# A larger share of gathered rows beside the kept blocks, and the gate's preparation spread over fifty blocks with gathers beside it

## The chip, the cores and the metric

The kernel runs on one core of one Trainium2 chip. The metric is the device time of one launch in microseconds (us); lower is better. A core has TensorE (PE in the rows), VectorE (DVE), ScalarE (ACT), GpSimd (POOL) and SyncE (SP). Each takes its own instructions strictly in order, and they meet through semaphores. Transfers issued by SP go through one queue, those issued by POOL through another, and both are served by the same 16 DMA engines.

## What is computed

One layer of an encoder for 512 tokens of width 1024, all in float32. The reference, cut to what matters here:

```python
h = h + mixed @ w_out                       # attention and recurrence, first part of the kernel
xn2 = rms_norm(h, norm_ffn_g)
# PEER: 8 heads pick 16 of 128 x 128 experts each, so 128 experts for a token
def block(args):
    xb, ib, gb = args
    ue = exp_u[ib]
    logits = jnp.einsum('td,tkd->tk', xb, ue)
    act = jax.nn.gelu(logits) * gb
    ve = exp_v[ib]
    return jnp.einsum('tk,tkd->td', act, ve)
h = h + peer(xn2)
xn3 = rms_norm(h, norm_ple_g)
gate = jax.nn.sigmoid(xn3 @ ple_w_gate)
h = h + gate * (p @ ple_w_proj)
out = rms_norm(h, final_norm_g)
```

## The kernel before

The tokens are four tiles of 128. The experts of the first three tiles are worked out densely: a loop over 128 blocks of 128 experts makes all logits (the U loop, line 1017), and a second loop over the 128 blocks adds up the values (the **V loop**, line 1174). The fourth tile is done by **rows**: for each of its tokens' 128 choices, POOL gathers one row of `exp_u` or `exp_v` for each of the 128 tokens (`gather`, line 893, an indirect transfer of 512 KB into a tile named `rr` or `xn`), and DVE either multiplies it with the tile's activations (a u row, line 926) or adds it to `h` (a v row, line 933). There are 128 u rows and 128 v rows, handed out by the generator `rows` in units of cost 1.15.

The work beside the loops is paced by objects of the class `Background`: `run(share)` adds the share to a debt and draws steps from a generator until the debt is used up. In the V loop `bg` is what is left of the rows, and `prep` is `prepare()`, which loads the gate's weights. One V block consists of:

- `v_prep` (line 1047), one block ahead: the block's weights are multiplied out (`am`, line 1057) and split into a high and a low part (`ah` on ACT, `al` on DVE, lines 89 and 91).
- the rows of `exp_v` for the block are loaded by SP (`r`), and split likewise into `rh` on ACT and `rl` on DVE.
- `v_mm`: 18 matmuls into the accumulators `acc`, three for each pair of parts (lines 96 to 98).
- a share of the background: 1.2 (`BG_V`), for the rows, or from block 60 (`PREP`) until it is done for `prep`, in place of the rows.

The pools give `rh`, `rl`, `ah` and `al` three buffers each, so DVE can be at most two blocks ahead of PE.

For 26 of the blocks (`KEEP`; in the V loop's order those at 6 to 31) the logits stay on chip. For the others `lg` is read back, 192 KB a block.

`prepare()` costs 19.9 units in all: 0.6, then the loads and splits of `pT` and `w_proj` (four tiles), eight small products `psp` of six matmuls each, and eight loads and splits of `w_gate`. Each load goes by POOL's queue into a tile `w` that takes one of the four `rr` buffers, the same that gathers use, and is split by ACT and then DVE into `wg` (line 91 again, called W below).

After the V loop each of the four tiles is finished by `finish` (line 1129): norm, transposes (`turn`), 48 gate matmuls of 512 columns or their equal, sigmoid, product, final norm, store. The fourth tile can start there only when its last row is added. `bg.run(1e9)` at line 1229 draws all rows that are left.

A scheduler sets the order of instructions on each engine when the kernel is built, and the chip follows that order.

Of the kernel before, what the change touches and what calls it, by code (L numbers as in the profile page):

```python
# [39 lines left out]
KEEP = 26  # L40
G_SCALE = 2.0 ** 14
RO_AT = [2, 1, 1, 1, 1, 1, 1, 0, 0, 1, 0, 0, 1, 0, 0, 1, 0, 0, 1, 1, 9]
TOP_FIRST, TOP_THEN, MAKE, SIDE_1, SIDE, BG_V, HOT_DVE, PREP, SIDE_2 = 2.2, 1.0, 0.5, 0.6, 1.2, 1.2, 4, 60, 2.1
LAST = 3
N_HOT = 13
N_AT = 15, 17, 17
# [13 lines left out]
def trunk(ctx, tc, x, xT, pT, pos, w_lru, w_qkv, w_out, w_q, keys, wab, w_gate, w_proj,  # L60
# [85 lines left out]
    with ExitStack() as st:  # L146
# [129 lines left out]
        for ct in range(8):  # L276
# [12 lines left out]
            if ct < 4:  # L289
# [16 lines left out]
                for da in range(4):  # L306
                    i = da * 4 + ct
# [677 lines left out]
    order = [(J0 + i) % P for i in range(P)]  # L985
    feed = [ut[j].rearrange("p k e -> p (k e)") for j in range(P)] + [v[j * P:(j + 1) * P, :] for j in order]
    ahead = []
    kept = {}

    def advance():  # L990
        while feed and len(ahead) < 3:
            ahead.append(row_load(feed.pop(0)))
# [24 lines left out]
    for j in range(P):  # L1017
# [3 lines left out]
        else:  # L1021
            if j == P - KEEP:
                top.run(1e9)
            i = j - (P - KEEP)
# [22 lines left out]
    def v_prep(i):  # L1047
        j = order[i]
        gj = gcs[i // JC][:, :, i % JC, :]
        lg = kept.get(j)  # L1050
        if lg is None:
            lg = up.tile([P, NU], F32, tag="lg", name="lg")
            nc.sync.dma_start(lg, ld[j])
        if i + JC < P:
            weights(i // JC + 1, i % JC, vp)
        am = vp.tile([P, NTB, TB], F32, tag="am", name="am", bufs=1)
        nc.vector.tensor_mul(am, lg.rearrange("p (b t) -> p b t", t=TB), gj)  # L1057
        am = am.rearrange("p b t -> p (b t)")
        ah = vp.tile([P, NV], R, tag="ah", name="ah", bufs=LAST)
        al = vp.tile([P, NV], R, tag="al", name="al", bufs=LAST)  # L1060
        split(am, ah, al)
        return ah, al

    def v_mm(i, t, vh, vl, ah, al):
        tt = slice(t * P, (t + 1) * P)
        for n in range(2):
            ns = slice(n * T, (n + 1) * T)
            mm3(acc[t][n], ah[:, tt], al[:, tt], vh[:, ns], vl[:, ns], i == 0, i == P - 1)
# [13 lines left out]
    def load_gains():  # L1082

        both = vp.tile([P, 2, D], F32, tag="gc", name="gains")
        gains.extend([both[:, 0, :], both[:, 1, :]])
        for i in range(2):
            nc.sync.dma_start(gains[i], row[:, 256 + (i + 1) * D:256 + (i + 2) * D].to_broadcast([P, D]))

    def prepare():
        late_room()  # L1090
        yield 0.6
        for t in range(NT):
            for n in range(2):
                ns = slice(n * T, (n + 1) * T)
                psp = psu.tile([P, T], F32, tag="psl", name="psp")

                ph, pl = wg4[0][:, 0:2, 0:T], wg4[2][:, 0:2, 0:T]
                wph, wpl = wg4[0][:, 2:4, :], wg4[2][:, 2:4, :]
                if t == 0 and n == 0:
                    got = []  # L1100
                    for k in range(2):
                        w = gp.tile([P, D], F32, tag="rr", name="w")
                        nc.gpsimd.dma_start(w[:, 0:T], pT[k * P:(k + 1) * P, :])
                        got.append((w[:, 0:T], ph[:, k, :], pl[:, k, :]))
                        w = gp.tile([P, D], F32, tag="rr", name="w")
                        nc.gpsimd.dma_start(w, w_proj[k * P:(k + 1) * P, :])
                        got.append((w, wph[:, k, :], wpl[:, k, :]))
                        yield 0.3
                    yield 1.2
                    for g_ in got:  # L1110
                        split(*g_)
                        yield 0.6
                    yield 0.6
                tt = slice(t * P, (t + 1) * P)
                for k in range(2):
                    mm3(psp, ph[:, k, tt], pl[:, k, tt], wph[:, k, ns], wpl[:, k, ns], k == 0, k == 1)
                nc.scalar.copy(pp[0][:, t, ns], psp)
                yield 0.5

        got = []  # L1120
        for k in range(DK + 3):
            if k < DK:
                got.append(gp.tile([P, D], F32, tag="rr", name="w"))
                nc.gpsimd.dma_start(got[k], w_gate[k * P:(k + 1) * P, :])
            if k >= 3:
                split(got[k - 3], wg(k - 3, 0), wg(k - 3, 1))
            yield 1.2 if k >= 3 else 0.3
# [41 lines left out]
    bg = Background(side.gen)  # L1169
    prep = Background(prepare())  # L1170
# [3 lines left out]
    for i in range(P - LAST + 1):  # L1174
        advance()
        if i + 1 < P:
            vn.append(v_prep(i + 1))
        if i == P - JC:
            load_gains()
        if i == P - LAST:  # L1180
            break
        rhl, ahl = ahead.pop(0), vn.pop(0)
        for t in range(ND_V):
            v_mm(i, t, *rhl, *ahl)
        if i >= PREP and not prep.done:
            prep.run(BG_V)
        else:
            bg.run(BG_V)
    for i in range(P - LAST + 2, P):
        vn.append(v_prep(i))  # L1190
    prep.run(1e9)
# [111 lines left out]
```

## Time and profile before

| | us |
|---|---|
| median of 3 runs (1502.62 to 1505.04) | 1504.44 |
| the profiled execution's own time | 1502.74 |
| its span, first to last instruction | 1501.0 |
| V loop on PE, first to last accumulating matmul | 898.47 to 1437.35 |
| after it, to the end of the span | 63.65 |

The profile is of one execution. Times in rows are counted from the start of the span; the share of busy time is an average over stages that differ. A timeline row gives the start, the duration, the engine, the line, what is written from what, and in brackets how long the engine was idle just before and what ended that.

### The profile page before, as it was taken

What the parts mean: (1) busy time and instruction counts of PE and PEld (TensorE: products, weight loads), DVE (VectorE), ACT (ScalarE), POOL (GpSimd) and SP (SyncE); (2) the same over time, 40 slices, a digit from 0 to 9 for tenths busy, and PEclk for the clock granted to TensorE, in tenths of its full rate; (3) what the DMA queues carried; (4) which work ended last, traced back from release to release, by engine and by line L of the source; (5) the groups of instructions that cost most, each with busy time, mean ns of one, the idle gap of its engine ahead of it and who ended that gap; (6) DMA issues with size and microseconds to landing.
All of it is one profiled execution on the core that took longest, in us unless ns stands there. A gap on an engine that the chain in (4) does not pass through costs nothing.

```text
span 1501.0 us, 22206 instructions
## 1 busy us (share of the span) xinstructions
PE 1464.1 (98%) x7907; PEld 1294.7 (86%) x7907; DVE 1257.0 (84%) x2481; ACT 741.1 (49%) x1059; POOL 428.6 (29%) x320
## 2 busy tenths in 40 slices
PE   8999999999899999999999989999999999999996
PEld 6887678899899999999999987888888888888875
DVE  7686987789999999999878757788887588878895
ACT  7974754354555654565455533333333453333345
POOL 0000000010223374235333344344443014344450
PEclk9999999999999999999999999999999999999998
DMA  7223022156789898889998799989999789999971
GB/s 257 61 94 127 15 86 88 43 195 229 239 294 335 285 347 327 305 296 345 370 330 300 266 321 340 321 300 328 360 373 359 248 280 351 366 353 357 322 227 64
DMA packets 169199, 394.21 MB, mean 263 GB/s; under 512 B 15360, under 2 KB 90880, under 8 KB 166016
## 3 DMA queue, kind: packets, MB, share of 16 engines
q1 hardware_dynamic: 112336, 207.52, 41.1%
q0 software_dynamic: 38464, 140.00, 26.4%
q10 hardware_dynamic: 18288, 45.27, 7.8%
q8 instruction: 62, 1.02, 0.3%
q14 instruction: 49, 0.40, 0.1%
HBM read 345.41 MB, written 47.32 MB: 262 GB/s over the span
## 4 chain that ended last, share of the span: by engine, by line
PE 66%; DVE 21%; ACT 4%; issue 4%; DMA 3%; SPq 1%; DVEq 0%; ACTq 0%
PE acc L98 11%; PE acc L97 11%; PE acc L96 11%; PE psl L96 6%; PE psl L97 6%; PE psl L98 6%; DVE rl L91 4%; PE pg L855 2%; DVE rr L926 2%; PE ps L96 2%; PE ps L98 2%; PE ps L97 2%; DVE h L933 1%; DMA r<-in_v_dram 1%; SPq L1000 1%
## 5 line engine op out<-in xcount | busy, mean ns | idle before, releaser
L89 ACT ACTIVATE rh<-r 128x1024 fp32r<-128x1024 f32 x256 | 270.8, 1059 | 423.1 <-PE psl L97 188.1
L91 DVE TENSOR_TENSOR rl<-r,rh 128x1024 fp32r<-128x1024 f32 x256 | 312.2, 1220 | 95.5 <-ACT rh L89 93.4
L96 PE MATMUL psl<-x2h,rh 128*128 128x384 f32 x1024 | 348.2, 340 | 7.4 <-ACT keep L660 5.0
L98 PE MATMUL psl<-x2h,rl 128*128 128x384 f32 x1024 | 344.3, 336 | 3.6 <-DVE rl L91 3.6
L97 PE MATMUL psl<-x2l,rh 128*128 128x384 f32 x1024 | 343.9, 336 | 0.0
L98 PE MATMUL acc<-rh,al 128*128 128x512 f32 x768 | 299.8, 390 | 1.1 <-DVE al L91 1.1
L96 PE MATMUL acc<-rh,ah 128*128 128x512 f32 x768 | 299.4, 390 | 0.7 <-ACT ah L89 0.7
L97 PE MATMUL acc<-rl,ah 128*128 128x512 f32 x768 | 299.4, 390 | 0.3 <-DVE rl L91 0.3
L894 POOL DMA_INDIRECT rr<-in_u_dram,qidx x84 | 123.0, 1465 | 382.0 <-DVE rl L91 180.7
L894 POOL DMA_INDIRECT rr<-in_v_dram,qidxv x82 | 150.8, 1839 | 187.7 <-DVE rl L91 163.9
L96 PEld LDWEIGHTS psl<-x2h,rh 128*128 128x128 f32 x1024 | 193.0, 189 | 8.9 <-ACT keep L660 5.3
L98 PEld LDWEIGHTS psl<-x2h,rl 128*128 128x128 f32 x1024 | 193.2, 189 | 4.6 <-DVE rl L91 4.5
L97 PEld LDWEIGHTS psl<-x2l,rh 128*128 128x128 f32 x1024 | 193.3, 189 | 0.0
L98 PEld LDWEIGHTS acc<-rh,al 128*128 128x128 f32 x768 | 144.5, 188 | 31.8 <-DVE al L91 1.9
L96 PEld LDWEIGHTS acc<-rh,ah 128*128 128x128 f32 x768 | 144.6, 188 | 31.2 <-ACT ah L89 1.1
L97 PEld LDWEIGHTS acc<-rl,ah 128*128 128x128 f32 x768 | 144.4, 188 | 30.6 <-DVE rl L91 0.7
L89 ACT ACTIVATE ah<-am 128x384 fp32r<-128x384 f32 x128 | 66.3, 518 | 94.9 <-DVE am L1057 61.5
L933 DVE SCALAR_TENSOR_TENSOR h<-rr,qg,h 128x1024 f32<-128x1024 f32 x82 | 104.9, 1279 | 3.7 <-DMA rr<-in_v_dram,qidxv 3.7
L926 DVE CUSTOM_DVE_ANT_0 rr<-rr,xn 128x1024 f32<-128x1024 f32 x84 | 102.1, 1217 | 6.0 <-DMA rr<-in_u_dram,qidx 6.0
L894 POOL DMA_INDIRECT xn<-in_u_dram,qidx x44 | 68.6, 1559 | 110.7 <-DVE rl L91 92.7
L894 POOL DMA_INDIRECT xn<-in_v_dram,qidxv x46 | 74.8, 1627 | 88.8 <-DVE rl L91 81.4
L858 ACT COPY sg<-pg 128x512 f32<-128x512 f32 x96 | 95.8, 1107 | 1.0 <-ACT sc L695 0.4
(342 smaller groups left out, 2275.5 us busy)
## 6 DMA issues: line engine op xcount, KB each, us to landing
r<-in_ut_dram SPq DMA_DIRECT2D x128, 512.0 KB, 4.8
r<-in_v_dram SPq DMA_DIRECT2D x128, 512.0 KB, 6.8
gd<-sg ACTq DMA_DIRECT2D x24, 1024.0 KB, 7.5
gc<-gd SPq DMA_DIRECT2D x128, 192.0 KB, 7.7
ld<-lg ACTq DMA_DIRECT2D x102, 192.0 KB, 5.0
lg<-ld SPq DMA_DIRECT2D x102, 192.0 KB, 6.3
w<-in_w_qkv_dram SPq DMA_DIRECT2D x12, 512.0 KB, 3.6
w<-in_w_out_dram SPq DMA_DIRECT2D x8, 512.0 KB, 3.8
```

The costliest lines, as they stand in the source:

```text
L89: nc.scalar.activation(hi, src, AF.Copy, scale=1.0 if scale is None else scale)
L91: return nc.vector.tensor_sub(lo, src, hi.bitcast(F32))
L96: nc.tensor.matmul(ps, lhsT=lh, rhs=rh, start=first, stop=False)
L97: nc.tensor.matmul(ps, lhsT=lh, rhs=rl, start=False, stop=False)
L98: nc.tensor.matmul(ps, lhsT=ll, rhs=rh, start=False, stop=last)
L855: nc.tensor.matmul(pg[:, i - q, :], lhsT=o1[:, i // 2, :, i % 2], rhs=o2[part][:, i // 2, :, i % 2], start=part == 0, stop=part == 1)
L858: nc.scalar.copy(sg[:, :, s0:s0 + 4].rearrange("p j t -> p t j"), pg)
L894: g = nc.gpsimd.indirect_dma_start(out=dst, out_offset=None, in_=table, in_offset=bass.IndirectOffsetOnAxis(ap=idx, axis=0))
L926: behind(nc.vector.tensor_tensor_reduce(rr, rr, xn[:, t, :], 1.0, 0.0, ALU.mult, ALU.add, act[:, k % 16:k % 16 + 1]))
L933: behind(nc.vector.scalar_tensor_tensor(h[:, t, :], rr, qg[:, t, k:k + 1], h[:, t, :], op0=ALU.mult, op1=ALU.add))
L1000: nc.sync.dma_start(gcs[-1][:, b0:b1], gd[b0:b1, :, j * TB:(j + JC) * TB].rearrange("b p (j t) -> p b j t", t=TB))
```

## The change

Three numbers and two calls change. The preparation begins at block 40 in place of 60, at a share of 0.4 a block in place of 1.2, and rows go on beside it at 1.0 a block. Beside blocks that are kept on chip the rows' share is 1.4 in place of 1.2.

```diff
-TOP_FIRST, TOP_THEN, MAKE, SIDE_1, SIDE, BG_V, HOT_DVE, PREP, SIDE_2 = 2.2, 1.0, 0.5, 0.6, 1.2, 1.2, 4, 60, 2.1
+TOP_FIRST, TOP_THEN, MAKE, SIDE_1, SIDE, BG_V, HOT_DVE, PREP, SIDE_2 = 2.2, 1.0, 0.5, 0.6, 1.2, 1.2, 4, 40, 2.1
+
+BG_K, BG_P, PREP_V = 1.4, 1.0, 0.4
...
         if i >= PREP and not prep.done:
-            prep.run(BG_V)
+            prep.run(PREP_V)
+            bg.run(BG_P)
         else:
-            bg.run(BG_V)
+
+            bg.run(BG_K if order[i] in kept else BG_V)
```

What this does to the order shows on POOL and DVE. Line numbers of the changed kernel are two higher than before.

POOL, from where the gate's weights are loaded, before (`w` are these loads, `rr` and `xn` gathered rows):

```order
L1103 DMA w<-in_pT_dram 128x512
L894 DMA xn<-in_u_dram,qidx 128x1024
L1106 DMA w<-in_w_proj_dram 128x1024
L1103 DMA w<-in_pT_dram 128x512
L1106 DMA w<-in_w_proj_dram 128x1024
L1124 DMA w<-in_w_gate_dram 128x1024 x8
L894 DMA rr<-in_u_dram,qidx 128x1024 x2
```

and after, the loads of `w_gate`:

```order
L1126 DMA w<-in_w_gate_dram 128x1024 x2
L896 DMA xn<-in_v_dram,qidxv 128x1024
L1126 DMA w<-in_w_gate_dram 128x1024 x2
L896 DMA rr<-in_v_dram,qidxv 128x1024
L1126 DMA w<-in_w_gate_dram 128x1024
L896 DMA rr<-in_v_dram,qidxv 128x1024 x3
L896 DMA xn<-in_v_dram,qidxv 128x1024 x2
L1126 DMA w<-in_w_gate_dram 128x1024
L896 DMA xn<-in_v_dram,qidxv 128x1024
L1126 DMA w<-in_w_gate_dram 128x1024
```

The loads moved in among gathers; `pT` and `w_proj`, not shown, stand 20 gathers earlier than these, four in a row.

DVE, where `w_gate` is split, before (blocks 71 to 73 of the V loop; a block begins with `am` and ends with `al`):

```order
L1057 TENSOR_TENSOR am<-lg,gc 128x384
L91 TENSOR_TENSOR rl<-r,rh 128x1024
L91 TENSOR_TENSOR wg_11666<-w,wg_11664 128x1024 x2
L91 TENSOR_TENSOR al<-am,ah 128x384
L1057 TENSOR_TENSOR am<-lg,gc 128x384
L91 TENSOR_TENSOR rl<-r,rh 128x1024
L91 TENSOR_TENSOR wg_11666<-w,wg_11664 128x1024 x2
L91 TENSOR_TENSOR al<-am,ah 128x384
L1057 TENSOR_TENSOR am<-lg,gc 128x384
L91 TENSOR_TENSOR rl<-r,rh 128x1024
L91 TENSOR_TENSOR wg_11667<-w,wg_11665 128x1024
L91 TENSOR_TENSOR al<-am,ah 128x384
```

and after (end of block 70, and block 71; `h<-` are v rows):

```order
L93 TENSOR_TENSOR wg_10962<-w,wg_10960 128x1024
L93 TENSOR_TENSOR rl<-r,rh 128x1024
L935 SCALAR_TENSOR_TENSOR h<-xn,qg,h 128x1024
L1059 TENSOR_TENSOR am<-lg,gc 128x384
L93 TENSOR_TENSOR wg_10962<-w,wg_10960 128x1024
L93 TENSOR_TENSOR wg_10963<-w,wg_10961 128x1024
L93 TENSOR_TENSOR rl<-r,rh 128x1024
L93 TENSOR_TENSOR al<-am,ah 128x384
```

The splits now stand in the same blocks as rows. Blocks 65 to 79 of before hold all eight `w_gate` splits and no row; after, blocks 68 to 79 hold the eight splits and twelve rows.

DVE, after the V loop's last `al`: 21 rows stood there, 7 stand there now. A part of that stretch before:

```order
L1161 TENSOR_REDUCE sm<-sm 128x1
L933 SCALAR_TENSOR_TENSOR h<-xn,qg,h 128x1024
L101 TENSOR_SCALAR sm<-sm 128x1
L933 SCALAR_TENSOR_TENSOR h<-xn,qg,h 128x1024
L1153 TENSOR_TENSOR sg<-sg,pp 128x512
L933 SCALAR_TENSOR_TENSOR h<-xn,qg,h 128x1024
L1154 TENSOR_TENSOR h<-h,sg 128x512
```

and of after, from its sixth and seventh (last) row, with the fourth tile's norm (the last L1137):

```order
L935 SCALAR_TENSOR_TENSOR h<-rr,qg,h 128x1024
L1137 SCALAR_TENSOR_TENSOR x_14265<-h,sm,gains 128x1024
L935 SCALAR_TENSOR_TENSOR h<-xn,qg,h 128x1024
L1155 TENSOR_TENSOR sg<-sg,pp 128x512
L1156 TENSOR_TENSOR h<-h,sg 128x512
L103 TENSOR_SCALAR sm<-sm 128x1
L105 RECIPROCAL sm<-sm 128x1
L1137 SCALAR_TENSOR_TENSOR x_14292<-h,sm,gains 128x1024
```

The fourth tile's norm and its transposes moved ahead of the gate matmuls of the second tile but four.

## Rows read from the trace of the kernel before

**Rows 1.** The profile's page: busy time, share of the span and instructions of an engine.

```profile
PE 1464.1 (98%) x7907; PEld 1294.7 (86%) x7907; DVE 1257.0 (84%) x2481; ACT 741.1 (49%) x1059; POOL 428.6 (29%) x320
```

**Rows 2.** Busy time of each engine in stretches of the V loop (the second and third hold the gate's preparation) and of the end; last columns: granted clock of TensorE, share of the 16 DMA engines, GB/s.

```profile
1050.00:1100.00 50.00, 50.00 (x222) 41.42 (x221) 44.59 (x55) 19.46 (x26) 22.14 (x13) 1.00 1.03 358
1150.00:1200.00 50.00, 50.00 (x222) 41.42 (x221) 28.55 (x37) 24.20 (x34) 3.21 (x6) 1.00 0.81 267
1200.00:1250.00 50.00, 50.00 (x222) 41.39 (x221) 40.05 (x54) 25.20 (x32) 10.56 (x9) 1.00 0.91 307
1470.00:1501.00 31.00, 18.17 (x95) 15.23 (x93) 14.90 (x32) 14.46 (x30) 0.00 (x0) 0.84 0.16 60
```

**Rows 3.** Timeline of PE after the V loop: the first gate matmul, the transposes of the third tile, the last gate matmul of the third tile, then the fourth tile's transposes, its first gate matmul, the first of its 256-column ones and its last.

```profile
1439.37 0.48 PE L96 MATMUL gate<-wg,hl 128*128 128x512 f32 x1
...
1450.37 1.03 PE L1141 MATMUL turn<-ident,x 128*128 128x128 f32 x8
...
1472.83 0.39 PE L98 MATMUL gate<-wg,hl 128*128 128x512 f32 x1
1476.21 1.09 PE L1141 MATMUL turn<-ident,x 128*128 128x128 f32 x8 [3.00 <-DVE x L1135]
1479.30 0.79 PE L96 MATMUL gate<-wg,hl 128*128 128x512 f32 x1 [2.00 <-DVE hl L91]
...
1487.24 0.28 PE L96 MATMUL gate<-wg,hl 128*128 128x256 f32 x1
...
1492.88 0.28 PE L98 MATMUL gate<-wg,hl 128*128 128x256 f32 x1
```

**Rows 4.** Timeline of DVE after the V loop: the seventh and the last (twenty-first) row added to the fourth tile, and that tile's norm. (The row of 1445.19 is two merged.)

```profile
1445.19 2.59 DVE L933 SCALAR_TENSOR_TENSOR h<-xn,qg,h 128x1024 f32<-128x1024 f32 x2
...
1469.22 1.28 DVE L933 SCALAR_TENSOR_TENSOR h<-xn,qg,h 128x1024 f32<-128x1024 f32 x1
...
1474.87 1.28 DVE L1135 SCALAR_TENSOR_TENSOR x<-h,sm,gains 128x1024 f32<-128x1024 f32 x1
```

**Rows 5.** Timeline of DVE in the V loop: one block's work with one row, and the beginning of the next.

```profile
957.61 0.56 DVE L1057 TENSOR_TENSOR am<-keep,gc 128x384 f32<-128x384 f32 x1
958.08 1.22 DVE L91 TENSOR_TENSOR rl<-r,rh 128x1024 fp32r<-128x1024 f32 x1
959.22 1.28 DVE L933 SCALAR_TENSOR_TENSOR h<-rr,qg,h 128x1024 f32<-128x1024 f32 x1
960.41 0.55 DVE L91 TENSOR_TENSOR al<-am,ah 128x384 fp32r<-128x384 f32 x1
961.00 0.56 DVE L1057 TENSOR_TENSOR am<-keep,gc 128x384 f32<-128x384 f32 x1
```

**Rows 6.** Timelines of DVE and PE, how far DVE is ahead: the `al` of block 57 and PE's first matmul of that block, the `rl` of block 76 and PE's first matmul of it, the `al` of block 80 and PE's first matmuls of blocks 80 and 81. (Blocks are counted on PE by 18 matmuls each from the first at 898.47.)

```profile
1131.13 0.55 DVE L91 TENSOR_TENSOR al<-am,ah 128x384 fp32r<-128x384 f32 x1
1135.66 0.39 PE L96 MATMUL acc<-rh,ah 128*128 128x512 f32 x1
...
1222.47 1.22 DVE L91 TENSOR_TENSOR rl<-r,rh 128x1024 fp32r<-128x1024 f32 x1
1224.06 0.39 PE L96 MATMUL acc<-rh,ah 128*128 128x512 f32 x1
...
1232.80 0.56 DVE L91 TENSOR_TENSOR al<-am,ah 128x384 fp32r<-128x384 f32 x1 [0.65 <-ACT ah L89]
1240.38 0.39 PE L96 MATMUL acc<-rh,ah 128*128 128x512 f32 x1
1244.46 0.39 PE L96 MATMUL acc<-rh,ah 128*128 128x512 f32 x1
```

**Rows 7.** Timelines of DVE, POOL and ACT: two loads of `w_gate` from the W whose end frees the buffer, over POOL's issue and ACT's split, to the next W.

```profile
1191.84 1.23 DVE L91 TENSOR_TENSOR wg<-w,wg 128x1024 fp32r<-128x1024 f32 x1 [0.27 <-ACT wg L89]
1193.36 0.53 POOL L1124 DMA_DIRECT2D w<-in_w_gate_dram  x1 [26.32 <-DVE wg L91]
1200.09 1.06 ACT L89 ACTIVATE wg<-w 128x1024 fp32r<-128x1024 f32 x1 [3.09 <-DMA w<-in_w_gate_dram]
1201.18 1.23 DVE L91 TENSOR_TENSOR wg<-w,wg 128x1024 fp32r<-128x1024 f32 x1 [2.81 <-ACT wg L89]
...
1202.70 0.53 POOL L1124 DMA_DIRECT2D w<-in_w_gate_dram  x1 [7.38 <-DVE wg L91]
1206.86 1.06 ACT L89 ACTIVATE wg<-w 128x1024 fp32r<-128x1024 f32 x1 [2.00 <-DMA w<-in_w_gate_dram]
1207.95 1.23 DVE L91 TENSOR_TENSOR wg<-w,wg 128x1024 fp32r<-128x1024 f32 x1 [1.00 <-ACT wg L89]
```

**Rows 8.** Waits from 898 to 1434, the V loop: us in total, times, longest.

```profile
DVE wg L91 <- ACT wg L89: 15.9, 9, 3.9
```

**Rows 9.** Transfers from 1130 to 1215, around the preparation: KB each, median us from issue to landing.

```profile
r<-in_v_dram SPq DMA_DIRECT2D x18, 512.0 KB, 5.4
w<-in_w_gate_dram POOLq DMA_DIRECT2D x8, 512.0 KB, 5.8
```

**Rows 10.** The same from 898 to 1130, with rows gathered all along.

```profile
r<-in_v_dram SPq DMA_DIRECT2D x56, 512.0 KB, 7.3
```

**Rows 11.** Timelines of DVE and POOL: the longest way round, the second W of a pair that frees a buffer, POOL's issue into it, and the W that splits what was loaded.

```profile
1193.27 1.23 DVE L91 TENSOR_TENSOR wg<-w,wg 128x1024 fp32r<-128x1024 f32 x1 [0.20 <-ACT wg L89]
1194.79 0.53 POOL L1124 DMA_DIRECT2D w<-in_w_gate_dram  x1 [0.90 <-DVE wg L91]
1203.53 1.23 DVE L91 TENSOR_TENSOR wg<-w,wg 128x1024 fp32r<-128x1024 f32 x1 [1.12 <-ACT wg L89]
```

## The prediction

> **What bounds the kernel now.** I read the page's busy times first: PE is busy for 98% of the span [rows 1], so time can be won only where PE is idle or slow, and is lost wherever PE is made to wait. Then the stretches [rows 2]: through the V loop PE is busy for all of every 50 us, before, in and after the gate's preparation, at full clock. Only at the end is it not: 18.2 of the last 31 us, at a mean granted clock of 0.84. So the V loop is bound by PE, at 4.08 us a block (1244.46 − 1240.38) [rows 6], and the end by something else. The end's timelines name it: PE waits 3.0 us for the fourth tile's norm and 2.0 us for the split of its transposes [rows 3], and that norm could not begin before the last of 21 leftover rows was added at 1470.5 [rows 4].
>
> **The end, what the change removes.** Rows drawn in the V loop's 125 paced blocks: before 108 × 1.2 = 129.6 units. The preparation costs 19.9 units, so at 0.4 it lasts 50 blocks (40 to 89). After: 26 kept × 1.4 + 49 × 1.2 + 50 × 1.0 = 145.2. The difference of 15.6 units is 13.6 rows at 1.15, and the order shows 14 fewer after the loop, 7 for 21. The seventh row ended at about 1446.5 before [rows 4], so the fourth tile's norm can start 24 us sooner. It does not bring 24 us, since PE has the other tiles' gates to do anyway. What is late next is PE itself: from its first gate matmul at 1439.37 it needs 144 matmuls of 512 columns for three tiles and 8 transposes, which before took until 1473.05 (1472.83 + 0.22) [rows 3]; then 1.0 for the fourth tile's transposes, 24 × 0.227 = 5.4 at full clock, and 48 × 0.12 = 5.8 (1487.24 to 1493.0) [rows 3]. That ends at 1485.3 where it was 1493.2, so **the end gains 7.9 us**: 5.0 of waits, 2.5 of slow clock (the first 24 matmuls took 1487.24 − 1479.30 = 7.9 for 5.4), and 0.4 of overlap. What follows the last matmul is the same. PE now meets the fourth tile's transposes after four of the second tile's gate matmuls, at about 1452; by DVE's and ACT's queue the norm is ready near 1451.6, a margin under a us. So the gain may be as little as 5, and at most 8.5.
>
> **The kept blocks at 1.4.** A block costs DVE `am` 0.47, `rl` 1.14, `al` 0.58 and 1.2 for a row (starts in [rows 5]): 2.2 + 1.2 × 1.4/1.15 = 3.65 of 4.08 us. DVE and PE's slack hide it, and a kept block reads 192 KB less of logits, against 89 KB more of rows. I cost it at 0, at most 1.
>
> **The preparation among rows, where the V loop may lose.** On average it fits: 2.2 + 0.87 rows × 1.2 + 13 us of W over 50 blocks = 3.5 of 4.08 us. But it comes in lumps, and DVE is in order. A W waits for its load, and the `rl` and `al` that PE needs stand behind it. DVE is never far ahead: 4.0 us with rows at full share (`al` of block 57 ended at 1131.68, PE began it at 1135.66), 7.0 at most, where it waits for buffers (block 80: 1233.36 against 1240.38) [rows 6]. Before, with no row at all beside the W, the `rl` of block 76 ended at 1223.69 and PE took it at 1224.06: 0.4 us was left [rows 6]. Waits for W came to 15.9 us there, nine times [rows 8]. The change puts a us of rows into each of those blocks.
>
> The way round a buffer is a chain: the instruction that frees it, POOL's issue, the landing, ACT's split, W. It took 8.1 us (1193.07 to 1201.18) and, the quickest, 5.5 (1202.41 to 1207.95) [rows 7]; the longest was 9.0 (1194.50 to 1203.53) [rows 11]. How much DVE work stands between the freeing instruction and W is read off the changed order; the rest is a wait. Three lumps:
>
> - A, from the `al` of block 44 to that of 46. Work: 2 `am`, 2 `al`, 2 `rl`, 2 rows, a W and half a one = 8.5. PE allows 4.0 + 2 × 4.08 = 12.1. Waits at 8.1: two, with 3.3 and 3.4 of work between: 9.5.
> - B, from the `al` of 67 to that of 71. Work: 4 `am`, 4 `al`, 6 `rl`, 4 rows, 5 W = 21.7. PE allows 7.0 + 4 × 4.08 = 23.3. Work between for the five: 2.2, 6.5, 8.6, 9.1, 5.7, so waits 5.9 + 1.6 + 0 + 0 + 2.4 = 9.9.
> - C, from the `al` of 71 to that of 79, DVE now with no lead. Work: 8 `am`, 8 `al`, 8 `rl`, 7 rows, 3 W = 29.3; PE allows 32.6. Waits: 3.6 for the first (4.5 between), none for the second, 4.4 for the last, whose load stands on POOL behind a gather.
>
> Waits 27.4, less slack 3.6 + 1.6 + 3.3 = 8.5: PE loses 18.9 us. At 5.5 a round the waits mostly vanish and it loses 2.4 (0.7 + 1.7 + 0); at 9.0, 25.6. Worked through in the same way for before, the twelve W come to 20.5 us of waits at 8.1, and the trace has 15.9 [rows 8], so the sum is too high by a quarter: 27.4 × 0.78 − 8.5 = 12.9. On the other side, loads land later when rows are gathered beside them: the `r` loads took 7.3 us with rows and 5.4 without [rows 9, 10]. **I take 15 us**, between 12.9 and 18.9, with 2.4 and 25.6 as ends. The eight small products are the same matmuls in other blocks, 0.
>
> A row gives 5.8 us for landing 512 KB by POOL's queue [rows 9]. The Trainium skill (DMA: Bandwidth & Descriptors, Anatomy of one DMA — SWDGE (gpsimd) path) has about 2.0 us plus the bytes over 436 KB per us, an estimate of 3.2 here. By that rule the way round would be 8.1 − 2.6 = 5.5 us and the V loop would lose 2.4 us, which is the first rival below; the trace does not bear it out while other queues are busy.
>
> **The sum.** 1502.74 of the profiled execution + 15 − 7.9 = 1509.8. The median of the runs lies 1.7 above the profiled one, so I predict **1511.5**.
>
> **Rivals.**
>
> - Loads return quickly, 5.5 us a round: the gaps between gathers leave them room, and DVE's lead covers the rest. The V loop loses 2.4, the end gains 7.9: 1504.4 − 5.5 = 1499, at best 1496.5. For it: one round of the three shown was that short [rows 7], and between the lumps DVE regains its lead at 0.6 us a block (4.08 − 3.5). Against it: at that moment no gather ran. It decides where PE loses less than 7.9.
> - Loss and gain cancel: 5 to 11 lost in the V loop, so 1502 to 1507. For it: the smaller of the two sums, 12.9, is not far, and a longer wait for one W brings the next load closer.
> - The 16 DMA engines are the bound: a block of the preparation moves 512 + 192 + 192 + 445 + 110 KB = 1451 KB in 4.08 us, 364 GB/s, where 358 GB/s filled them [rows 2]. Rounds of 9.0 and `r` late as well, and each stall followed by matmuls at the lower clock, as at the end (2.5 us): 25.6 + some 3 − 7.9 = 1525.
> - The change does not do what it says, rows still hold the end: excluded by the order, with 7 rows left.
>
> **Chances.** Forecast (PE loses 11 to 25): 0.60. Third rival: 0.10. Loss and gain cancel: 0.15. First rival: 0.15. The range 1499 to 1521 takes in the forecast's bounds and the most of the first two rivals, and leaves out the third and the best of the first. A measurement of this kernel tells about 0.2%, 3 us, from no change: slower by more than that 0.70, within it 0.15, faster 0.15.
>
> **What would show it.** In the changed profile PE no longer waits for the fourth tile's norm, its gate matmuls run without a break from the first tile's to the fourth's, and the time from the V loop's last matmul to the end is about 56 for 63.65. PE's busy share falls in three places of the V loop, near blocks 46, 71 and 79, with `rl` and `al` as what ended its waits, and DVE waits before W there for 4 to 6 us at a time. It is wrong if PE stays busy throughout from block 40 to 90; then the time is the first rival's.

## The result: 1525.21 us, and the profile after

The changed kernel takes 1525.21 us (median of 5 runs, 1519.05 to 1527.83), the kernel before 1504.36 beside it: a ratio of 1.0133 (95% interval 1.0117 to 1.0149). The profiled execution took 1527.83 us, with a span of 1526.1. In the profiles the time splits in two at the V loop's last matmul:

| | V loop, first to last `acc` matmul | PE busy in it | PE idle in it | from there to the end |
|---|---|---|---|---|
| before | 538.9 | 536.7 | 2.2 | 63.65 |
| after | 570.4 | 548.8 | 21.6 | 55.8 |

The V loop lost 31.6 us, of which 19.5 are waits of PE and 12.1 are longer matmuls; the end gave back 7.85. The two profiled executions are 25.1 us apart and the medians 20.85, so some 4 us of what the profiles show is not in most executions.

Stretches after, columns as in [rows 2]; the first line is the whole V loop:

```profile
899.85:1470.29 570.44, 548.82 (x2363) 446.48 (x2363) 452.49 (x594) 210.81 (x285) 219.67 (x143) 0.98 0.93 324
...
1050.00:1100.00 50.00, 47.61 (x205) 37.69 (x203) 38.60 (x47) 18.57 (x25) 18.90 (x14) 1.00 0.92 330
1150.00:1200.00 50.00, 50.00 (x222) 41.44 (x221) 30.05 (x43) 18.75 (x26) 13.24 (x10) 1.00 0.88 292
1200.00:1250.00 50.00, 45.25 (x187) 36.45 (x187) 38.63 (x47) 20.97 (x27) 15.34 (x15) 0.93 0.93 328
1250.00:1300.00 50.00, 41.48 (x169) 32.71 (x168) 36.51 (x46) 15.81 (x22) 16.59 (x11) 0.93 0.84 272
1490.00:1526.00 36.00, 28.25 (x148) 24.20 (x146) 15.62 (x31) 15.95 (x33) 0.00 (x0) 0.96 0.16 59
```

Where [rows 2] had 50.00 of 50 us on PE, three stretches now fall short. Counted block by block (18 matmuls each, 4.08 us at best), blocks 43 to 48 lose 6.1 us, 70 and 71 lose 7.9, and 77 to 79 lose 12.2; the other 5 us lie at blocks 3, 4, 27, 36 and 125, outside the preparation's splits. In the worst stretch the DMA engines moved 272 GB/s at a share of 0.84, less than elsewhere: over the stretch they were not full (e3 settles it). The granted clock, between its levels of 1.2 and 2.4 GHz, falls with the waits: 0.93 of full speed in the two stretches from 1200 on, where before it was 1.00 up to 1250 [rows 2].

Waits of the V loop after (us in total, times, longest):

```profile
ACT wg L91 <- DMA w<-in_w_gate_dram: 29.7, 8, 8.9
DVE wg L93 <- ACT wg L91: 23.0, 6, 7.3
...
PE acc L98 <- ACT ah L91: 13.8, 6, 6.4
...
PE acc L100 <- DVE al L93: 5.2, 7, 1.2
```

W's waits grew from 15.9 us to 23.0 [rows 8], the longest from 3.9 to 7.3. What ended most of PE's waits is `ah`, not `rl` and `al`. The longest wait, by the timelines of POOL, ACT, DVE and PE, shows why:

```profile
1249.72 1.22 DVE L93 TENSOR_TENSOR rl<-r,rh 128x1024 fp32r<-128x1024 f32 x1
1251.21 1.74 POOL L896 DMA_INDIRECT rr<-in_v_dram,qidxv  x1 [3.80 <-DVE rl L93]
1252.95 0.58 POOL L1126 DMA_DIRECT2D w<-in_w_gate_dram  x1
1254.01 1.04 POOL L896 DMA_INDIRECT rr<-in_v_dram,qidxv  x1 [0.47 <-DVE rl L93]
1262.08 1.06 ACT L91 ACTIVATE wg<-w 128x1024 fp32r<-128x1024 f32 x1 [8.91 <-DMA w<-in_w_gate_dram]
1263.16 1.23 DVE L93 TENSOR_TENSOR wg<-w,wg 128x1024 fp32r<-128x1024 f32 x1 [7.29 <-ACT wg L91]
1263.98 0.51 ACT L91 ACTIVATE ah<-am 128x384 fp32r<-128x384 f32 x1
1264.54 0.80 PE L98 MATMUL acc<-rh,ah 128*128 128x512 f32 x1 [6.36 <-ACT ah L91]
```

The last load of `w_gate` stands on POOL right behind a gather that waited for `rl`; 9.1 us later ACT can split it. Until then ACT stands still too, with `rh` and `ah` of block 79 behind the split, as DVE stands with `rl` and `al`.

The end: busy times from the last `acc` matmul on, before and after; then the timeline of PE after, the fourth tile's transposes and the last gate matmul.

```profile
1437.35:1501.00 63.65, 49.65 (x241) 41.28 (x238) 47.39 (x71) 32.89 (x59) 14.79 (x11) 0.92 0.38 126
1470.30:1526.00 55.70, 46.82 (x240) 39.59 (x238) 31.69 (x57) 30.43 (x57) 0.00 (x0) 0.97 0.10 38
...
1485.12 1.04 PE L1143 MATMUL turn<-ident,x 128*128 128x128 f32 x8
...
1517.97 0.28 PE L100 MATMUL gate<-wg,hl 128*128 128x256 f32 x1
```

The transposes that waited 3.0 us [rows 3] now wait for nothing and stand among the other tiles' gates; PE is idle for 8.9 us behind the loop, where it was for 14.0.

### The profile page after: what moved, and what is told of

It reads as the page before. It is cut to its first block, busy times and chain, and to the rows that moved or that the text cites. A ratio compares the mean times of both kernels' runs of the same rounds, so it can differ in the third digit from the quotient of the medians.

```text
span 1526.1 us, 22171 instructions
## 1 busy us (share of the span) xinstructions
PE 1473.4 (97%) x7907; PEld 1296.8 (85%) x7907; DVE 1257.7 (82%) x2481; ACT 737.9 (48%) x1057; POOL 429.5 (28%) x320
## 5 line engine op out<-in xcount | busy, mean ns | idle before, releaser
L98 PE MATMUL acc<-rh,ah 128*128 128x512 f32 x768 | 302.7, 394 | 14.3 <-ACT ah L91 13.8
L100 PE MATMUL acc<-rh,al 128*128 128x512 f32 x768 | 303.2, 395 | 5.2 <-DVE al L93 5.2
L99 PE MATMUL acc<-rl,ah 128*128 128x512 f32 x768 | 302.6, 394 | 2.1 <-DVE rl L93 1.9
L93 DVE TENSOR_TENSOR al<-am,ah 128x384 fp32r<-128x384 f32 x128 | 70.9, 554 | 32.2 <-ACT ah L91 29.4
```

Source lines behind the costliest of these rows:

```text
L93: return nc.vector.tensor_sub(lo, src, hi.bitcast(F32))
L98: nc.tensor.matmul(ps, lhsT=lh, rhs=rh, start=first, stop=False)
L99: nc.tensor.matmul(ps, lhsT=lh, rhs=rl, start=False, stop=False)
L100: nc.tensor.matmul(ps, lhsT=ll, rhs=rh, start=False, stop=last)
```

## The experiments

Theory 1: a split of the preparation waits on ACT and DVE until its load is back, and PE's operands stand behind it. Theory 2: the DMA engines are full. Theory 3: the work on DVE alone is too much. The columns behind the ratio are those of one profiled execution of each run; the table is read run by run below.

| run | median us | ratio to before (95%) | V loop | PE idle in it | end |
|---|---|---|---|---|---|
| e1, kept share alone, from 60 | 1517.94 | 1.0070 to 1.0104 | 560.0 | 15.2 | 58.1 |
| e2, spread alone | 1512.46 | 1.0030 to 1.0066 | 555.3 | 11.9 | 56.4 |
| e3, splits wait for no load | 1509.05 | 1.0016 to 1.0047 | 547.2 | 7.2 | 55.9 |
| e4, loads ahead | 1510.98 | 1.0033 to 1.0065 | 549.2 | 9.2 | 55.8 |
| e5, kept share alone, from 62 | 1499.14 | 0.9958 to 0.9985 | 544.9 | 7.3 | 56.3 |
| e6, before, from 58 | 1516.76 | 1.0066 to 1.0129 | 552.5 | 12.5 | 66.1 |
| e7, loads ahead, no rows beside | 1510.09 | 1.0028 to 1.0059 | 550.2 | 10.1 | 56.3 |
| e8, 1.4 in all blocks, from 63 | 1511.02 | 1.0032 to 1.0066 | 556.0 | 12.2 | 55.5 |
| e9, after, from 42 | 1522.02 | 1.0100 to 1.0150 | 568.3 | 19.9 | 55.8 |
| e10, loads ahead, held, kept 1.2 | 1506.69 | 1.0013 to 1.0043 | 551.8 | 10.6 | 56.3 |
| e11, kept share 1.3, from 60 | 1501.39 | 0.9966 to 0.9994 | 541.4 | 5.1 | 60.8 |
| e12, gathers not held | 1521.00 | 1.0111 to 1.0158 | 563.2 | 15.6 | 55.8 |
| e13, loads on SP's queue | 1515.58 | 1.0060 to 1.0135 | 561.2 | 16.2 | 55.6 |

**e1, the kept share alone.** Against the changed kernel:

```
-HOT_DVE, PREP, SIDE_2 = ..., 4, 40, 2.1
+HOT_DVE, PREP, SIDE_2 = ..., 4, 60, 2.1
...
-            prep.run(PREP_V)
-            bg.run(BG_P)
+            prep.run(BG_V)
```

> The kept blocks' share of 1.4 alone; the gate is prepared as before, from block 60 on, with no gathered row beside it. Theory 1 (a split of the preparation stands on VectorE until its load has come back, and rl and al stand behind it): nothing of that is touched, so the V loop from the first to the last acc matmul stays at 538.5 us, within 1, and the end gives back a part of the 7.85 us that the full change gave there, since some 4 of the 14 rows that the full change took out of the end go: 3 to 8 us, a time of 1497 to 1501 us. If instead the larger share in the kept blocks is itself a part of the loss, the loop is longer by some us and the time stays at 1504 or above.

By its time the second reading, but not in the way that it meant: the loop lost 21 us, 15.5 of them in one place, blocks 80 to 85, not all along as a share that is too large would. (Blocks 80 and 81 took 14.1 and 13.3 us, of which 10.9 are the eight small products, which came there too.) POOL's timeline there:

```profile
1224.15 1.68 POOL L896 DMA_INDIRECT xn<-in_v_dram,qidxv  x1 [68.61 <-DVE rl L93]
1225.83 0.61 POOL L1105 DMA_DIRECT2D w<-in_pT_dram  x1
```

Where the kernel before issued its first load of `pT` at 1144.76, here it waited behind a gather that was held for 68.6 us, until rows went on; then all twelve splits came in a heap. I formed a fourth theory: rows and loads share a ring, and where the rows stop its phase decides whether a load finds an `rr`.

**e2, the spread alone.** Against the changed kernel:

```
-BG_K, BG_P, PREP_V = 1.4, 1.0, 0.4
+BG_K, BG_P, PREP_V = 1.2, 1.0, 0.4
```

> The preparation spread out as in the changed kernel, the kept blocks back at 1.2. Theory 1: the V loop keeps its whole loss, 570 us within 2 for 538.5, and the end keeps most of its gain, so 1524 to 1528 us. If the kept share is a part of the loss, the loop is shorter than 568 us by what it cost.

The loop lost 16.4 us, about half of the whole. The kept share was thus a part of the loss, by the second reading of the expectation, though it has no instruction in the lumps: blocks 43 to 46 lost 4.6 us, 73 and 74 5.7, 81 and 82 5.0, all at splits, as in the changed kernel but each smaller. That the two halves come to about the whole (13.9 and 8.5 us above before for 20.9) is chance: most of e1's loss is a heap at blocks 80 to 85, which the changed kernel does not have.

**e3, splits that wait for no load.**

```
-                        got.append((w[:, 0:T], ph[:, k, :], pl[:, k, :]))
+                        got.append((xn[:, 3, 0:T], ph[:, k, :], pl[:, k, :]))
...
-                        got.append((w, wph[:, k, :], wpl[:, k, :]))
+                        got.append((xn[:, 3, :], wph[:, k, :], wpl[:, k, :]))
...
-                split(got[k - 3], wg(k - 3, 0), wg(k - 3, 1))
+                split(xn[:, 3, :], wg(k - 3, 0), wg(k - 3, 1))
```

> The changed kernel with all its loads of pT, w_proj and w_gate in place and in the same buffers, but each split reads a tile of xn that has long been on the chip, so that no split waits for its load (the gate and the projection are computed from other numbers). The DMA traffic and the work of ScalarE and VectorE are those of the changed kernel. Theory 1 (the wait for the load's way round): lumps at blocks 44 to 48, 70 to 71 and 77 to 79 go, all but some 3 us; the V loop takes 541 to 548 us for 570, and the time is 1497 to 1505 us. Theory 2 (the 16 DMA engines are full, so that r comes late): the loop stays within 5 us of 570 and the time is 1520 or above. Theory 3 (VectorE's work in a lump of splits and rows is more than its lead bears): the raw work of the lumps less what passes leaves 59.5 for 68 us at the most, so nearly nothing or as much as now; the time is 1518 or above.

The loop took 547.2 us, 23 less than after, with the same traffic and work; blocks 43 to 49 and 70 to 79 run at 4.08 us each. The run changed one thing more than it meant to: the loads stayed near their blocks (42 to 79), but the splits, bound to no load, moved up in the order, eight to blocks 25 to 33 and four to 65 and 66, still among rows. A stretch of 50 us, DVE's timeline at block 65, and PE's waits in the loop:

```profile
1200.00:1250.00 50.00, 50.00 (x223) 41.39 (x222) 38.31 (x48) 18.37 (x24) 17.71 (x15) 1.00 1.04 371
...
1178.45 3.49 DVE L93 TENSOR_TENSOR wg<-xn,wg 128x1024 fp32r<-128x1024 f32 x3
1181.86 1.22 DVE L93 TENSOR_TENSOR rl<-r,rh 128x1024 fp32r<-128x1024 f32 x1
1182.99 1.22 DVE L928 CUSTOM_DVE_ANT_0 rr<-rr,xn 128x1024 f32<-128x1024 f32 x1
...
PE acc L98 <- ACT ah L91: 3.5, 2, 2.5
PE acc L100 <- DVE al L93: 2.0, 3, 1.1
PE acc L99 <- DVE rl L93: 1.6, 4, 0.7
```

Theory 2 falls for the lumps: with the loads there and the DMA engines at 371 GB/s, a share of 1.04, PE lost nothing from 1200 to 1250. Theory 3 falls too, though not in the same blocks: four splits and two rows within blocks 65 and 66 cost PE nothing, and all twelve at most some 3 us (blocks 25 to 27 and 35). Theory 1 is what is left, and the timelines after show it at work.

The median, 1509.05, is above the range that I gave. The executions reach from 1502.8 to 1512.4 and the profiled one has a span of 1501.8, so some 6 us of most of them are in no trace.

**e4, the loads ahead in places of their own.** For `w_gate`; `pT` and `w_proj` likewise:

```
...
-                got.append(gp.tile([P, D], F32, tag="rr", name="w"))
-                nc.gpsimd.dma_start(got[k], w_gate[k * P:(k + 1) * P, :])
+            if k < 4:
+                nc.gpsimd.dma_start(wg(k, 1), w_gate[k * P:(k + 1) * P, :].bitcast(R))
+            c = (k + 4) % DK
+            split(wg(c, 1).bitcast(F32), wg(c, 0), wg(c, 1))
```

> A mend: the changed kernel with the loads of the preparation put straight into the places of the low halves and split there in place, so that they need no rr buffer; w_gate's rows 4 to 7 are loaded before the projection's matmuls, rows 0 to 3 while rows 4 to 7 are split. Each load so has four steps of the preparation to come back in, and the gathers keep all their rr buffers. Theory 1: no split waits for more than 1 us, the V loop takes 541 to 548 us and the end keeps the 7.85 us, so 1497 to 1505 us. Theories 2 and 3: the traffic and the work are the same, so the loop stays above 560 us and the time above 1515.

A miss in the time, 1510.98, but the loop won 21 us back and the three lumps are gone. Eight of the splits moved up too, to blocks 25 to 35. What the loop still lost, 10 us more than before, lies at blocks 3 and 4 (5.4 us more than the 4.4 that they lose before) and 31 to 36 (4.7): free of the ring, the loads moved up to the start of the V loop. POOL's timeline, first and third of them:

```profile
902.74 0.61 POOL L1110 DMA_DIRECT2D wg<-in_w_gate_dram  x1
...
908.93 0.60 POOL L1110 DMA_DIRECT2D wg<-in_w_gate_dram  x1
```

and the waits from 905 to 935, where ACT then waited 12.7 us for one `r`, for 8.5 before:

```profile
ACT rh L91 <- DMA r<-in_v_dram: 13.1, 2, 12.7
```

**e5, the kept share alone from block 62.** Against e1:

```
-HOT_DVE, PREP, SIDE_2 = ..., 4, 60, 2.1
+HOT_DVE, PREP, SIDE_2 = ..., 4, 62, 2.1
```

> The kept blocks' share of 1.4 alone, as in the run of the kept share alone, but the preparation begins at block 62 instead of 60; nothing else. A fourth theory, formed after that run: rows go round a ring of seven buffers, four rr and three slices of xn, and the loads of the preparation take rr alone. Where the rows stop, the place in the ring decides how many rr still hold a gathered row; with all four held no load can start before rows go on, so in that run the first load of pT went out at 1225.83 us, behind a gather that POOL had waited 68.6 us for, and ten splits then stood in five blocks. With block 62 the program stands as in the kernel before, two blocks later. Theory 4: the V loop takes 538 to 541 us, the end gives 3 to 8 us, the time is 1496 to 1502 us. If the larger share itself overdraws VectorE or the DMA engines: a loop of 555 us or more and a time above 1512.

The phase theory's time: 1499.14 us, faster than both kernels (ratio 0.9971). The first load of `pT` went out at 1154.90, in the stretch without rows. The end gained 7.3 of the 7.85 us. The loop was 6 us longer, 4 more than I gave, in small waits: at blocks 11, 27 and 52 behind an `r` that ACT had waited for (7.3, 6.2 and 4.9 us), at 12 and 20, and at 64 and 65 (2.8 us) behind splits of the preparation. PE's waits:

```profile
PE acc L100 <- DVE al L93: 3.8, 4, 1.1
PE acc L98 <- ACT ah L91: 2.4, 2, 1.4
PE acc L99 <- DVE rl L93: 0.9, 2, 0.5
```

**e6, the kernel before from block 58.** Against the kernel before:

```
-HOT_DVE, PREP, SIDE_2 = ..., 4, 60, 2.1
+HOT_DVE, PREP, SIDE_2 = ..., 4, 58, 2.1
```

> The kernel before with one number changed: the preparation begins at block 58 instead of 60. Theory 4 (the place in the ring of seven): at 58 all four rr are held where the rows stop, and the splits stand in a heap at blocks 80 to 82, so the V loop loses 16 to 24 us to that and the time is 1518 to 1528 us, with no share changed. If the place in the ring is not the cause: 1504 us within 3.

1516.76 us, just under the range I gave and 13 above before: no share changed, yet the heap is there (blocks 78 and 79 took 15.1 and 12.4 us, of which 10.9 are the small products; 78 to 82 lost 11.8), with the same mark on POOL:

```profile
1211.78 1.68 POOL L894 DMA_INDIRECT xn<-in_u_dram,qidx  x1 [72.06 <-DVE rl L91]
1213.46 0.61 POOL L1103 DMA_DIRECT2D w<-in_pT_dram  x1
```

In the program's order the heap stands for starts at 57, 58, 64 and 65 of those from 54 to 66, and comes back after seven: the ring has seven buffers. The phase is shown by e5 and e6, and e7 adds that without the ring the heap is gone; which buffers were held is argued from the order.

**e7, loads ahead with no rows beside.** Against e4, which has the changed kernel's 40:

```
-HOT_DVE, PREP, SIDE_2 = ..., 4, 40, 2.1
+HOT_DVE, PREP, SIDE_2 = ..., 4, 60, 2.1
...
-            prep.run(PREP_V)
-            bg.run(BG_P)
+            prep.run(BG_V)
```

> Kept blocks' share 1.4, the loads straight into the places of the low halves as in the run with the loads ahead, so that they need no rr, and the preparation from block 60 with no row beside it. Theories 1 and 4: no load waits for a ring's buffer, no split for its load; the V loop takes 540 to 548 us and the end gives 3 to 8 us, a time of 1498 to 1508 us. If the lumps come from work on VectorE alone, they stay: above 1512.

A miss: 1510.09. With e1's shares and e1's start, blocks 60 to 80 lost nothing but the small products, so the heap needed the ring. But the early loads cost as in e4: blocks 3 and 4 took 9.6 and 8.4 us (before 4.9 and 7.7), 31 to 33 lost 4.6.

**e8, 1.4 in all blocks.** Against e1:

```
-HOT_DVE, PREP, SIDE_2 = ..., 4, 60, 2.1
+HOT_DVE, PREP, SIDE_2 = ..., 4, 63, 2.1
...
-            bg.run(BG_K if order[i] in kept else BG_V)
+            bg.run(BG_K)
```

> The share of 1.4 in all blocks of the V loop and not in the kept ones alone; the preparation as in the kernel before, with no row beside it, from block 63 on, where the ring stands as it does in the kernel before at 60. Only 2 rows are left behind the last al. Theory 4, with VectorE's work at 2.2 + 1.22 x 1.2 = 3.7 us of 4.08 a block: the loop takes 538 to 545 us, the end gives all of the 7.85 us or a little more, and the time is 1493 to 1502 us, the fastest so far. If a share of 1.4 overdraws the lead over PE or the DMA engines (512 KB for the row, 192 or 0 KB for lg, 1.2 x 512 KB gathered): stalls all along the loop, above 1508 us.

The other reading: the loop lost 17 us all along (blocks 51, 52, 60, 92, 100, 107, 108). At each of these blocks PE's wait stands behind an `r` that ACT had waited for; ACT waited 134.5 us for `r` in all, before 89.3, and the stretch from 1050 to 1100 moved 374 GB/s at a share of 1.03, for 358 at 1.03 before [rows 2]. So the row share does meet theory 2: kept share 1.2, 1.3 and 1.4, and 1.4 everywhere, give loops of 538.9, 541.4, 544.9 and 556.0 us.

**e9, the changed kernel from block 42.**

```
-HOT_DVE, PREP, SIDE_2 = ..., 4, 40, 2.1
+HOT_DVE, PREP, SIDE_2 = ..., 4, 42, 2.1
```

> The changed kernel with one number changed: the spread preparation begins at block 42 instead of 40. The program then has the splits one by one, between al and the next rl of blocks 68, 69, 70, 71, 73, 76, 78 and 84, where the changed kernel has them in heaps behind al of 70 and 77. Theory 4 (the heaps come from the place in the ring of seven at which the loads ask for an rr, not from the shares): the V loop loses less than half as much, 545 to 556 us for 570, and the time is 1502 to 1514 us. If the spread as such costs it (rows and splits together more than VectorE or the DMA engines bear): 1520 us or above, as the changed kernel.

A miss, 1522.02: splits one by one cost as much as in heaps. The phase explains the heap where rows stop, not the spread. The timelines of POOL, ACT and DVE show a round:

```profile
1225.24 0.59 POOL L1126 DMA_DIRECT2D w<-in_w_gate_dram  x1
1232.87 1.06 ACT L91 ACTIVATE wg<-w 128x1024 fp32r<-128x1024 f32 x1 [6.76 <-DMA w<-in_w_gate_dram]
1233.97 1.23 DVE L93 TENSOR_TENSOR wg<-w,wg 128x1024 fp32r<-128x1024 f32 x1 [5.07 <-ACT wg L91]
1235.11 1.22 DVE L93 TENSOR_TENSOR rl<-r,rh 128x1024 fp32r<-128x1024 f32 x1
1236.60 1.74 POOL L896 DMA_INDIRECT rr<-in_v_dram,qidxv  x1 [7.92 <-DVE rl L93]
1238.34 0.58 POOL L1126 DMA_DIRECT2D w<-in_w_gate_dram  x1
```

W waits for its load, `rl` stands behind W, a gather is held for `rl`, and the next load stands behind that gather. The next W waited 5.97 us.

**e10, loads ahead, held behind `rl`.** Against e4, for each of the loads:

```
-BG_K, BG_P, PREP_V = 1.4, 1.0, 0.4
+BG_K, BG_P, PREP_V = 1.2, 1.0, 0.4
...
+        g = nc.gpsimd.dma_start(dst, src)
+        tc.add_manual_dep(g.ins, pace[-1].ins.name,
+                          mybir.DependencyInfo(mybir.DependencyClass.Sync, mybir.DependencyReason.DATA), reason="pace")
```

> The loads straight into the places of the low halves, as in the runs with the loads ahead, but each held behind the rl of its block, as the gathers are, since without that the order had five of the splits as early as blocks 25 to 31, where the DMA engines are full. Kept blocks at 1.2, the preparation spread from block 40 with rows beside it at 1.0. Theories 1 and 4: no heap beyond VectorE's own overdraw (2.2 + 1.23 + 1.28 = 4.7 for 4.08 us in some eight blocks, 5 us less its lead): the V loop takes 539 to 546 us, the end gives 6 to 8 us, a time of 1496 to 1506 us. If loads beside rows cost in themselves: above 1510.

1506.69, above the range by 0.7, with a loop of 551.8 us for 539 to 546. The second half of the preparation lost only 2.1 us (blocks 75 to 77), though its four splits still waited, 0.7, 3.5, 3.1 and 3.7 us, one to every third block: only the last of them cost PE anything. But blocks 45 and 46 lost 8.4, where ACT still waited 4.8 us for `pT` and 6.3 for `w_gate`. It does not beat before.

**e11, kept share 1.3.** Against e1; by the order the loads can start at 60 here:

```
-BG_K, BG_P, PREP_V = 1.4, 1.0, 0.4
+BG_K, BG_P, PREP_V = 1.3, 1.0, 0.4
```

> The kept share at 1.3, halfway; the preparation as before, with no row beside it, from block 60, where the ring lets the loads start. Against the run at 1.4 from block 62, which lost 6 us in the loop by stalls of 0.4 to 1.4 us for r at blocks 11, 12, 20, 27 and 52 and gained 7.4 us at the end: if those stalls are the DMA engines' (theory 2 for the rows, not for the preparation), half the extra rows cost 2 to 4 us and the end gives 3 to 6 us, a time of 1497 to 1503 us. If they are chance, the loop is within 2 us of 538.9 and the time 1496 to 1500 us.

1501.39: the loop lost 2.6 us and the end gave 2.8, just under its range. The loop and the time are those of theory 2 for the rows, though an effect this small is near what one profile can tell.

**e12, gathers no longer held.**

```
-BG_K, BG_P, PREP_V = 1.4, 1.0, 0.4
+PACED, BG_K, BG_P, PREP_V = 166,  1.4, 1.0, 0.4
...
-        tc.add_manual_dep(g.ins, pace[-1].ins.name,
+        if len(pace) < PACED:
+            tc.add_manual_dep(g.ins, pace[-1].ins.name,
```

> The changed kernel, but from the 166th row load on (V block 38) the gathers are no longer held until rl of their block and wait for their buffer alone; VectorE's order is nearly that of the changed kernel. Theory 5 (closed loop: split, rl behind it, gather held for that rl, next load behind that gather on POOL's queue, next split): the loads go out earlier and the V loop loses half or less, 545 to 556 us for 570, a time of 1502 to 1514 us. If the ring's buffers come free too late anyway: 565 us or more and a time above 1518.

At most a small part: in the profiles the V loop won 7 us of 31.6 (W waited 14.1 us for 23.0), under the half that I asked for. The time, 1521.00 (1518.8 to 1527.1), does not tell it from the changed kernel's 1519.1 to 1527.8, so a gain is not shown. The loads of `w_gate` now waited for a row to free their `rr` instead, by POOL's waits:

```profile
POOL w L1127 <- DVE h L936: 22.0, 4, 11.8
```

**e13, the loads on SP's queue.** For `pT`, `w_proj` and `w_gate`:

```
-                nc.gpsimd.dma_start(got[k], w_gate[k * P:(k + 1) * P, :])
+                nc.sync.dma_start(got[k], w_gate[k * P:(k + 1) * P, :])
```

> The changed kernel with the twelve loads of the preparation issued on SP's queue instead of POOL's. There they stand behind loads of r, which wait for an r that rl frees, so the loop of theory 5 is closed in the same way: 1515 to 1528 us. If only the gathers on POOL's queue hold them back: the loop loses half or less, below 1514 us.

1515.58, 10 us better than after, 12 worse than before. Timelines of SP, ACT and DVE:

```profile
1243.94 0.50 SPq L1126 DMA_DIRECT2D w<-in_w_gate_dram  x1
1251.44 1.06 ACT L91 ACTIVATE wg<-w 128x1024 fp32r<-128x1024 f32 x1 [5.69 <-DMA w<-in_w_gate_dram]
1252.53 1.23 DVE L93 TENSOR_TENSOR wg<-w,wg 128x1024 fp32r<-128x1024 f32 x1 [4.07 <-ACT wg L91]
```

From issue to ACT's split this last load took 7.5 us, for 9.1 on POOL's queue, and W waited 4.1 us for 7.3. The loop won 9.2 us of 31.6: the first reading by its range, at the edge, with a part of the second. So neither queue cures it. That the rest comes from the order, which with a load in an `rr` puts its split one way round behind the issue, is argued.

## Why the prediction was wrong

- **The direction and the place were right.** Slower, by waits of W near blocks 46, 71 and 79, for loads of the preparation. The timelines show the wait, and in e3, without it, the lumps are gone.
- **The end was right**, in size and in mechanism: 55.8 us as forecast, a gain of 7.85 for 7.9. PE's idle time there fell by 5 us, the 5.0 of waits, and its busy time by 2.8, for 2.9 of slow clock and overlap. e5 adds that the first few rows bring nearly all of it: 7.3 us with the kept share alone, which leaves 16 rows for 21.
- **The step that failed is "I take 15 us".** The V loop lost 31.6. Of the 16.6 us between, 12.1 are a term that the sum had at nothing, and 4.5 are waits of PE: more than priced in lump C, less in A and B, and some 2 us at blocks 4, 27 and 125, outside the preparation.
- **The term left out is what follows a wait.** The same matmuls took 12.1 us longer in the V loop. In lump C PE was idle for 8.5 of the 12.2 us lost and the rest is longer matmuls, at a granted clock of 0.86; in lump B 4.75 of 7.9, at 0.79. I had counted that for the end (2.5 us) and for the third rival ("some 3"), not for the forecast. Not all of the 12.1 is shown to be clock: in lump A the clock reads 1.00 and matmuls still took 2.2 us more.
- **Lump C was priced too low.** W waited 11.9 us in it for 8.0, and PE 8.5 for 4.7. The last wait was priced at 4.4 us and was 7.3: I had seen that the load stands behind a gather, and priced its way round like the others, 8.1 from the freeing instruction to W. Here the issue alone was 10.2 us before W (1252.95 to 1263.16), of which 9.1 went by until ACT could split, for 6.7 in the round of 8.1 [rows 7].
- **Lumps A and B came out right by luck.** They lost 6.1 and 7.9 us for 5.9 and 8.3, but W waited 6.3 and 4.8 us in them where the sum has 9.5 and 9.9, and PE 3.9 and 4.75; the longer matmuls made up the difference. So the discount to 0.78 was not the error: W's waits came to 23.0 us of the 27.4, 0.84.
- **DVE was named, ACT was not.** Most of PE's waits, 13.8 of 21.6 us, were for `ah`, held on ACT by the other half of the same split.
- **"The kept blocks at 1.4: 0, at most 1" was too small.** It left out that `r` comes later: alone the share costs 6 us in the loop (e5, some 3 of them at the preparation's splits), 2.6 at 1.3 (e11). In the changed kernel it also made the lumps larger (e2), in a way that the runs do not take apart.
- **The rivals.** The third gave 1525, the measured time, by another mechanism: the DMA engines were at 0.84 in the worst stretch, and e3 had the same traffic without the lumps. The first, quick loads, is out: ACT began its eight splits of `w_gate` 4.0 to 9.1 us after the issue, 6.2 in the median, where the quick round had 4.2 (1202.70 to 1206.86) [rows 7]. The Trainium skill's figures (DMA: Bandwidth & Descriptors, Anatomy of one DMA — SWDGE (gpsimd) path), an estimate of 3.2 us for such a load on POOL's queue, are not borne out beside gathers.

What stays open: the 6 us by which most executions of e3 and e4 are slower than the profiled ones, why the kept share enlarges the lumps, and how much of the 12.1 us is clock.

## What to carry to other kernels

Before work that loads is put beside a stream, ask what the load shares with it: a ring of buffers, an in-order queue, a release held for pacing; each ties the load's issue to the stream's progress, and its full way round lands on every engine that runs in order behind the split. Where a helper takes buffers from a ring at the place where a stream pauses, try its start at each block of one ring's length: two blocks' shift was worth 19 us here (e1 against e5), more than any share. And price a stall with what follows it: per 1 us that PE waited in the changed loop's lumps B and C it lost another 0.5 (13.3 us of waits, 6.8 of longer matmuls).

## What the runs showed that I had not expected

- A preparation may be displaced by seventeen blocks by its start alone (first split in block 78 for 61, e6): POOL stood for 68.6 and 72.1 us behind one held gather (e1, e6).
- The V loop has almost no room in the transfers either: at 1.4 everywhere `r` was waited for 134.5 us by ACT for 89.3 before and the loop took 17 us more.
- Loads set free of a ring are not issued where they stand in the code but as early as their places are free, 175 us sooner (902.74 for 1078.23 when held), and there ACT waited 12.7 us for an `r`, for 8.5 before.
